# A transpose of 8192 x 8192 floats: ranges begun one step apart, TensorE's steps as a loop, neighbouring copies merged

## The chip, the cores and the metric

The kernel runs on one core of a Trainium2 chip. The metric is the device time in microseconds (us). Each execution lists its time, the core's span (first to last instruction) and the share of the TensorE clock that was granted.

## The reference

```python
x = np.random.randn(8192, 8192).astype(np.float32)
def reference(x):
    return np.transpose(x)
```

It reads 268 MB and writes 268 MB. There is no arithmetic, so the work is moving bytes: in, turned by TensorE in 128 x 128 blocks, out.

## The kernel before

The matrix is cut into two strips of 4096 columns. A step takes 128 rows of a strip: one load of 2 MB (16 KB in each of 128 partitions), 32 transposes into PSUM (the memory that TensorE writes its results to, here eight banks), and copies from there into output registers, which are SBUF buffers of 2 MB. The strip has eight ranges of 512 columns. A range fills one register with the blocks of eight steps, so that a store writes rows of 4 KB. There are three input buffers and nine registers: eight are being filled, and one or two are on their way to memory.

```python
S = 32; B = 4; W = 8; NR = S // B     # 8 ranges of 4 blocks; 8 steps fill a register
NIN = 3; NREG = 9; NPS = 8
nc.alloc_sbuf_tensor("pad", [P, 32], dt)                 # 128 bytes, never used
pss = [nc.alloc_psum_tensor(f"ps{k}", [P, B * P], dt).ap() for k in range(NPS)]
...
for t, (s, c) in enumerate(chunks):
    nc.tensor.wait_ge(s_ld[t % NIN], 16 * (t // NIN + 1))
    for q in [(c + k) % NR for k in range(NR)]:          # the turn: a new register comes last
        if q not in window:
            end = min(c + (q - c) % W, CH - 1)           # a window never crosses a strip's end
            r = free.pop(0)
            ...  # the copying engine waits until register r has been stored
        if bank[n % NPS] is not None:
            nc.tensor.wait_ge(*bank[n % NPS])            # one of eight banks
        ...  # 4 transposes into ps, then one copy of 128x512 on ScalarE or VectorE
    for q, e, count in closing:
        ...  # wait for the copy, then store the register
    if t + NIN < len(chunks):
        nc.sync.wait_ge(s_pe, n)
        load(t + NIN)                                    # the load goes out after the store
```

The turn puts the range that needs a newly returned register last in its step. PSUM is handed back bank by bank. In the queue of DMA transfers each step's store goes ahead of the next load.

## Time and profile before

| reading | value | view |
|---|---|---|
| time, median of 3 | 1268.06 us (1265.97 to 1268.59) | times |
| span of the profiled run | 1265.1 us | page |
| busy: TensorE, VectorE, ScalarE | 722.6, 353.5, 300.7 us | page, part 1 |
| a packet of 16 KB on one DMA engine | 611 ns | packet records |
| a 2 MB load, a 2 MB store, issue to landing (the last of its 16 completion records) | 23.5, 22.7 us | page, part 6 |

The first lines are from the page of the kernel before: TensorE's busy time, DMA share and rate in 40 slices of the span, and the packets that bring instructions.

```profile
PE 722.6 (57%) x4096; PEld 690.6 (55%) x4096; DVE 353.5 (28%) x512; ACT 300.7 (24%) x513; POOL 0.7 (0%) x6
...
DMA  9999999999999999999999999999999999999998
GB/s 380 418 428 427 428 429 428 427 428 428 426 428 429 426 428 430 429 428 428 428 417 428 428 427 428 431 429 429 429 428 428 430 428 430 429 429 429 428 428 353
...
q8 instruction: 32, 0.52, 0.2%
```

DMA is at 9 tenths or more nearly to the end, while TensorE has 43% of the span left. Sixteen engines at 16,384 bytes in 611 ns make 429.0 GB/s. I use that as the full rate. The **loss** of a stretch is its length minus its bytes divided by the full rate, from the packet records (instruction packets are not counted as bytes moved). It comes out a little below zero where packets overlap.

Next, the windows view of the kernel before. Columns: stretch in us; its length; busy time (and instructions) of TensorE, its weight loads, VectorE, ScalarE and GpSimd; granted clock; DMA share; GB/s.

```profile
0.00:50.00 50.00, 32.62 (x224) 31.70 (x224) 18.71 (x28) 17.49 (x29) 0.70 (x6) 0.90 0.97 393
50.00:600.00 550.00, 319.98 (x1792) 306.70 (x1792) 155.50 (x225) 131.21 (x224) 0.00 (x0) 0.75 1.01 428
600.00:700.00 100.00, 55.66 (x320) 50.94 (x320) 27.14 (x40) 23.14 (x40) 0.00 (x0) 0.69 1.01 425
850.00:1150.00 300.00, 175.18 (x989) 167.82 (x987) 85.77 (x124) 72.64 (x124) 0.00 (x0) 0.76 1.01 429
1150.00:1240.00 90.00, 52.61 (x288) 50.48 (x288) 24.90 (x36) 21.09 (x36) 0.00 (x0) 0.73 1.01 429
```

And its last ten microseconds:

```profile
1255.00:1260.00 5.00, 0.00 (x0) 0.00 (x0) 0.00 (x0) 0.00 (x0) 0.00 (x0) 0.50 0.80 323
1260.00:1265.00 5.00, 0.00 (x0) 0.00 (x0) 0.00 (x0) 0.00 (x0) 0.00 (x0) 0.50 0.22 87
```

The rate is 428 to 429 GB/s except at the start, around the change of strips (600 to 700 us) and at the end, where the share falls to 0.80 and 0.22 because the sixteen engines don't finish together. In the middle TensorE waits for loads, as the waits view says (who waited for whom: us in total, times, longest):

```profile
PE ps L131 <- DMA in<-in_x_dram: 499.7, 124, 8.3
...
ACT reg L142 <- DMA out_dram<-reg: 33.8, 6, 13.5
DVE reg L144 <- DMA out_dram<-reg: 33.4, 5, 18.1
```

The queue is deep. The DMA part of the page gives issues, their size, and the median us from issue to landing; at 4.9 us for 2 MB, 23 us is nearly five transfers:

```profile
in<-in_x_dram SPq DMA_DIRECT2D x128, 2048.0 KB, 23.5
out_dram<-reg SPq DMA_DIRECT2D x114, 2048.0 KB, 22.7
```

One step on the timeline of the kernel before (start, length, engine, instruction, and in brackets the idle time before it and what ended it):

```profile
383.82 0.34 SPq L98 DMA_DIRECT2D in<-in_x_dram  x1
...
388.16 6.06 PE L131 MATMUL ps<-ident,in 128*128 128x128 f32 x32 [4.37 <-DMA in<-in_x_dram]
...
390.04 0.55 SPq L28 DMA_DIRECT2D out_dram<-reg  x1
...
394.25 0.34 SPq L98 DMA_DIRECT2D in<-in_x_dram  x1
```

A load lands, TensorE starts at once, the step's store is issued 1.9 us later and the next load when TensorE is done.

### The profile page before, as it was taken

Reading aid. Unit: us, or ns where it says so; the run is one execution under the profiler, and the core shown is the slowest. Engines: PE = TensorE matmul, PEld = TensorE weight load, DVE = VectorE, ACT = ScalarE, POOL = GpSimd, SP = SyncE. Lnnn points to the kernel's source line nnn. Section 1 sums busy time; section 2 is a strip of 40 time slices with the busy share of each in tenths; the row PEclk is TensorE's granted clock in tenths of the full one; section 3 lists DMA queues with packets and bytes.
Section 4 is the critical chain, followed back from the end, with each engine's and each line's share of the span. In section 5 each row is a group of like instructions: output and inputs, shape, how many; then the busy total and the mean of one; then the engine's idle time right before and its main releaser. Section 6 shows DMA issues by size and latency. Waiting matters only on the chain.

```text
span 1265.1 us, 9814 instructions
## 1 busy us (share of the span) xinstructions
PE 722.6 (57%) x4096; PEld 690.6 (55%) x4096; DVE 353.5 (28%) x512; ACT 300.7 (24%) x513; POOL 0.7 (0%) x6
## 2 busy tenths in 40 slices
PE   6555656665556555565456655656566555665651
PEld 6555645555456555564455555655455555565551
DVE  3322222322223222232133322223223222232220
ACT  3322222222222222222122222222222222222220
POOL 0000000000000000000000000000000000000000
PEclk8877686777776877768667777686867877777675
DMA  9999999999999999999999999999999999999998
GB/s 380 418 428 427 428 429 428 427 428 428 426 428 429 426 428 430 429 428 428 428 417 428 428 427 428 431 429 429 429 428 428 430 428 430 429 429 429 428 428 353
DMA packets 39308, 537.51 MB, mean 425 GB/s; under 512 B 4320, under 2 KB 4832, under 8 KB 6240
## 3 DMA queue, kind: packets, MB, share of 16 engines
q1 hardware_dynamic: 39264, 536.89, 100.0%
q8 instruction: 32, 0.52, 0.2%
q14 instruction: 12, 0.10, 0.0%
HBM read 268.44 MB, written 268.44 MB: 424 GB/s over the span
## 4 chain that ended last, share of the span: by engine, by line
DMA 78%; PE 20%; issue 0%; DVE 0%; ACT 0%; SPq 0%; ACTq 0%
DMA in<-in_x_dram 75%; PE ps L131 20%; DMA out_dram<-reg 2%; DVE reg L144 0%; ACT reg L142 0%; SPq L197 0%; SPq L68 0%; ACTq L140 0%
## 5 line engine op out<-in xcount | busy, mean ns | idle before, releaser
L131 PE MATMUL ps<-ident,in 128*128 128x128 f32 x4096 | 722.6, 359 | 514.8 <-DMA in<-in_x_dram 499.7
L131 PEld LDWEIGHTS ps<-ident,in 128*128 128x128 f32 x4096 | 690.6, 193 | 546.5 <-DMA in<-in_x_dram 520.8
L144 DVE COPY reg<-ps 128x512 f32<-128x512 f32 x512 | 353.5, 692 | 884.2 <-PE ps L131 850.8
L142 ACT COPY reg<-ps 128x512 f32<-128x512 f32 x512 | 299.4, 586 | 936.5 <-PE ps L131 902.7
L142 ACT ACT_TABLE_LOAD x1 | 1.3, 1283 | 0.9 <-SPq L68 0.9
L83 POOL TENSOR_SCALAR_AFFINE_SELECT ident<-ident 128x128 f32<-128x128 f32 x1 | 0.3, 292 | 0.2 <-POOL ident L81 0.2
L81 POOL MEMSET ident<- 128x128 f32 x1 | 0.2, 204 | 0.5 <-SPq L68 0.5
L186 POOL MEMSET const-bfloat16-1.0<- 128x1 bf16 x1 | 0.1, 101 | 0.0
L186 POOL MEMSET const-uint8-127<- 128x1 uint8 x1 | 0.1, 101 | 0.0
L186 POOL MEMSET const-float32-0.0<- 128x1 f32 x1 | 0.1, 98 | 0.2 <-issue 0.2
L186 POOL MEMSET const-float32-1.0<- 128x1 f32 x1 | 0.1, 98 | 0.0
## 6 DMA issues: line engine op xcount, KB each, us to landing
in<-in_x_dram SPq DMA_DIRECT2D x128, 2048.0 KB, 23.5
out_dram<-reg SPq DMA_DIRECT2D x114, 2048.0 KB, 22.7
out_dram<-reg SPq DMA_DIRECT2D x4, 1792.0 KB, 20.1
out_dram<-reg SPq DMA_DIRECT2D x4, 1536.0 KB, 19.2
out_dram<-reg SPq DMA_DIRECT2D x4, 1280.0 KB, 19.1
out_dram<-reg SPq DMA_DIRECT2D x4, 1024.0 KB, 17.9
out_dram<-reg SPq DMA_DIRECT2D x4, 768.0 KB, 16.3
out_dram<-reg SPq DMA_DIRECT2D x4, 512.0 KB, 13.2
```

Source lines behind the costliest of these rows:

```text
L81: nc.gpsimd.memset(ident, 0.0).then_inc(s_id, 1)
L83: nc.gpsimd.affine_select(out=ident, in_=ident, compare_op=mybir.AluOpType.not_equal, fill=1.0, base=0, pattern=[[-1, P]], channel_multipl ...
L131: last = nc.tensor.transpose(ps[:, b * P:(b + 1) * P], ins[t % NIN][:, (q * B + b) * P:(q * B + b + 1) * P], ident,)
L142: cp = nc.scalar.copy(out=o, in_=i)
L144: cp = nc.vector.tensor_copy(out=o, in_=i)
L186: nc = _bacc.Bacc("TRN2", target_bir_lowering=False, num_devices=1)
```

## The change

The intent: before, all ranges restart at the head of a strip, so that TensorE runs short of work at the seam and short stores pile up there. Now range q begins q steps after range 0 and takes its rows round (the last ones at the head of the strip), so that the strips join without a seam. TensorE's program becomes a loop of three steps. Copies of neighbouring ranges become one instruction. The core of the diff (cuts marked):

```diff
-        nc.alloc_sbuf_tensor("pad", [P, 32], dt)
-        pss = [nc.alloc_psum_tensor(f"ps{k}", [P, B * P], dt).ap() for k in range(NPS)]
+        pss = [nc.alloc_psum_tensor(f"ps{h}", [P, NH * R], dt).ap() for h in range(2)]
...
+    for t in range(T):                       # T = 2 * 64 + 7 steps
+        at = sorted(((t - q) // CH, q) for q in range(NR) if t >= q)
+        active.append([a for a in at if a[0] < NS])
...
+    EARLY = 2 * NIN                          # the first six loads have a place each
+    after = [None] * EARLY + [2, 4, 5] + list(range(6, T))
+    order = [("L", t) for t in range(9)]
+    for t in range(6, T):
+        if t + NIN < T:
+            order.append(("L", t + NIN))     # the load now goes ahead of the step's store
+        if closing[t]:
+            order.append(("S", t))
...
+        def transposes(t):
+            ...
+            for h in range((n + NH - 1) // NH):          # halves of four ranges, in column order
+                if used[h]:
+                    nc.tensor.sem_inc(s_bank[h], -1).wait_op(s_bank[h], 1, "sem-ge")
+                ...                                      # up to 16 transposes into half h
+        with nc.Fori(0, len(full) // NIN, engines=[nc.tensor.engine]):
+            for t in range(first, first + NIN):
+                transposes(t)
...
+                eng = (nc.scalar, nc.vector)[h]          # half 0: ScalarE, half 1: VectorE
+                ...                                      # one copy for up to four ranges
```

PSUM is now two halves of four banks. A half goes back to TensorE when all of its copies are done.

More of the change, by code (lines that the diff above doesn't have):

```diff
@@ L56 @@
     dt = x.dtype
-    S = 32
     B = 4
-    W = 8
-    NR = S // B
+    NR = 8
+    NH = NR // 2
     NIN = 3
-    NREG = 9
-    NPS = 8
+    NREG = NR + 1
     CH = N // P
-    J = S * P
+    R = B * P
+    J = NR * R
+    NS = M // J
+    T = NS * CH + NR - 1
+    SIZE = NR * R
+    active = []
+    for t in range(T):
+        at = sorted(((t - q) // CH, q) for q in range(NR) if t >= q)
+        active.append([a for a in at if a[0] < NS])
+    window_of = {}
+    closing = [None] * T
+    for s in range(NS):
+        for q in range(NR):
+            for t0 in range(s * CH + q, s * CH + q + CH, NR):
+                t1 = t0 + NR - 1
+                parts = []
+                a = t0
+                for t in range(t0, t1 + 1):
+                    if t == t1 or (t + 1) % CH == 0:
+                        parts.append((a, t))
+                        a = t + 1
+                w = {"col": s * J + q * R, "t0": t0, "t1": t1, "parts": parts}
+                closing[t1] = w
+                for t in range(t0, t1 + 1):
+                    window_of[t, s, q] = w
@@ new lines @@
+    free = list(range(NREG))
+    stored = [0] * NREG
+    for t in range(T):
+        for a in active[t]:
+            w = window_of[(t, *a)]
+            if w["t0"] == t:
+                w["reg"] = free.pop(0)
+                w["before"] = stored[w["reg"]]
+        if closing[t]:
+            stored[closing[t]["reg"]] += len(closing[t]["parts"])
+            free.append(closing[t]["reg"])
+    EARLY = 2 * NIN
+    after = [None] * EARLY + [2, 4, 5] + list(range(6, T))
+    order = [("L", t) for t in range(9)]
@@ L68 @@
+    for t in range(6, T):
+        if t + NIN < T:
+            order.append(("L", t + NIN))
+        if closing[t]:
+            order.append(("S", t))
     with tc.tile_critical():
-        nc.alloc_sbuf_tensor("pad", [P, 32], dt)
         ident = nc.alloc_sbuf_tensor("ident", [P, P], dt).ap()
         ins = [nc.alloc_sbuf_tensor(f"in{k}", [P, J], dt).ap() for k in range(NIN)]
-        regs = [nc.alloc_sbuf_tensor(f"reg{k}", [P, B * W * P], dt).ap() for k in range(NREG)]
-        pss = [nc.alloc_psum_tensor(f"ps{k}", [P, B * P], dt).ap() for k in range(NPS)]
+        regs = nc.alloc_sbuf_tensor("regs", [P, NREG * SIZE], dt).ap()
+        pss = [nc.alloc_psum_tensor(f"ps{h}", [P, NH * R], dt).ap() for h in range(2)]
@@ L75, with home @@
         s_id = nc.alloc_semaphore("s_id")
+        s_early = [nc.alloc_semaphore(f"s_early{t}") for t in range(EARLY)]
         s_ld = [nc.alloc_semaphore(f"s_ld{k}") for k in range(NIN)]
         s_st = [nc.alloc_semaphore(f"s_st{k}") for k in range(NREG)]
+        s_bank = [nc.alloc_semaphore(f"s_bank{h}") for h in range(2)]
         s_pe = nc.alloc_semaphore("s_pe")
         s_cp = [nc.alloc_semaphore("s_cpa"), nc.alloc_semaphore("s_cpv")]
+        def home(t):
+            buf, off = [
+                (ins[0], 0), (ins[0], R), (ins[0], 3 * R), (regs, (NREG - 1) * SIZE),
+                (ins[1], 0), (ins[2], 0),
+            ][t] if t < EARLY else (ins[t % NIN], 0)
+            return buf[:, off:off + len(active[t]) * R]
@@ L91 @@
         ).then_inc(s_id, 1)
-        nc.tensor.wait_ge(s_id, 2)
-        chunks = [(s, c) for s in range(M // J) for c in range(CH)]
-        def load(t):
-            s, c = chunks[t]
-            nc.sync.dma_start(
-                out=ins[t % NIN], in_=x[c * P:(c + 1) * P, s * J:(s + 1) * J]
-            ).then_inc(s_ld[t % NIN], 16)
-        for t in range(NIN):
-            load(t)
-        n = 0
-        copied = [0, 0]
-        bank = [None] * NPS
-        free = list(range(NREG))
-        stored = [0] * NREG
@@ L110 @@
-        window = {}
-        stores = 0
-        for t, (s, c) in enumerate(chunks):
-            nc.tensor.wait_ge(s_ld[t % NIN], 16 * (t // NIN + 1))
-            closing = []
-            for q in [(c + k) % NR for k in range(NR)]:
-                if q not in window:
-                    end = min(c + (q - c) % W, CH - 1)
-                    r = free.pop(0)
-                    window[q] = (c, end, r)
-                    if stored[r]:
-                        (nc.scalar, nc.vector)[q % 2].wait_ge(s_st[r], 16 * stored[r])
-                c0, end, r = window[q]
-                rows = (end - c0 + 1) * P
-                view = regs[r][:, :B * rows].rearrange("p (b i) -> p b i", b=B)
-                ps = pss[n % NPS]
-                e = q % 2
-                if bank[n % NPS] is not None:
-                    nc.tensor.wait_ge(*bank[n % NPS])
-                for b in range(B):
-                    last = nc.tensor.transpose(
-                        ps[:, b * P:(b + 1) * P],
-                        ins[t % NIN][:, (q * B + b) * P:(q * B + b + 1) * P],
+        used = [False, False]
@@ new lines, in transposes @@
+        def transposes(t):
+            if t < EARLY:
+                nc.tensor.wait_ge(s_early[t], 16)
+            else:
+                nc.tensor.sem_inc(s_ld[t % NIN], -16).wait_op(s_ld[t % NIN], 16, "sem-ge")
+            src = home(t)
+            n = len(active[t])
+            for h in range((n + NH - 1) // NH):
+                if used[h]:
+                    nc.tensor.sem_inc(s_bank[h], -1).wait_op(s_bank[h], 1, "sem-ge")
+                used[h] = True
+                for b in range(min(NH, n - h * NH) * B):
+                    tr = nc.tensor.transpose(
+                        pss[h][:, b * P:(b + 1) * P],
+                        src[:, h * NH * R + b * P:h * NH * R + (b + 1) * P],
@@ L134 @@
                         ident,
                     )
-                last.then_inc(s_pe, 1)
-                n += 1
-                o = view[:, :, (c - c0) * P:(c - c0 + 1) * P]
-                i = ps.rearrange("p (b i) -> p b i", b=B)
-                (nc.scalar, nc.vector)[e].wait_ge(s_pe, n)
-                if e == 0:
-                    cp = nc.scalar.copy(out=o, in_=i)
-                else:
-                    cp = nc.vector.tensor_copy(out=o, in_=i)
-                cp.then_inc(s_cp[e], 1)
@@ L146 @@
-                copied[e] += 1
-                bank[(n - 1) % NPS] = (s_cp[e], copied[e])
-                if c == end:
-                    closing.append((q, e, copied[e]))
-            for q, e, count in closing:
-                c0, end, r = window.pop(q)
-                rows = (end - c0 + 1) * P
-                j0 = s * J + q * B * P
-                dst = out[j0:j0 + B * P, c0 * P:c0 * P + rows]
-                dst = dst.rearrange("(b q) i -> q b i", q=P)
-                nc.sync.wait_ge(s_cp[e], count)
-                if stores:
-                    st = wide_dma(nc, nc.sync, "qSPDynamicHW", dst, regs[r][:, :B * rows])
-                else:
-                    st = nc.sync.dma_start(
-                        out=dst, in_=regs[r][:, :B * rows].rearrange("q (b i) -> q b i", b=B)
-                    )
-                st.then_inc(s_st[r], 16)
-                stores += 1
-                stored[r] += 1
-                free.append(r)
@@ L167 @@
-            if t + NIN < len(chunks):
-                nc.sync.wait_ge(s_pe, n)
-                load(t + NIN)
+                tr.then_inc(s_pe, 1)
+        nc.tensor.wait_ge(s_id, 2)
+        full = [t for t in range(T) if len(active[t]) == NR]
+        first = full[0] + len(full) % NIN
+        for t in range(first):
+            transposes(t)
+        with nc.Fori(0, len(full) // NIN, engines=[nc.tensor.engine]):
+            for t in range(first, first + NIN):
+                transposes(t)
@@ new lines @@
+        for t in range(full[-1] + 1, T):
+            transposes(t)
+        n = 0
+        done = []
+        copied = [0, 0]
+        final = [max(t for t in range(T) if len(active[t]) > h * NH) for h in range(2)]
+        over = []
+        for t in range(T):
+            for h in range((len(active[t]) + NH - 1) // NH):
+                eng = (nc.scalar, nc.vector)[h]
+                ws = [window_of[(t, *a)] for a in active[t][h * NH:(h + 1) * NH]]
+                place = []
+                for w in ws:
+                    if w["t0"] == t and w["before"]:
+                        eng.wait_ge(s_st[w["reg"]], 16 * w["before"])
+                    a, z = next(p for p in w["parts"] if p[0] <= t <= p[1])
+                    off = w["reg"] * SIZE + (a - w["t0"]) * R + (t - a) * P
+                    place.append((off, (z - a + 1) * P))
+                runs = []
+                for g in range(len(ws)):
+                    if runs:
+                        u = runs[-1]
+                        d = place[g][0] - place[g - 1][0]
+                        if place[g][1] == place[u[0]][1] and abs(d) < 2 ** 15 and (
+                            len(u) == 1 or d == place[u[1]][0] - place[u[0]][0]
+                        ):
+                            u.append(g)
+                            continue
+                    runs.append([g])
+                ends = [w is closing[t] for w in ws]
+                if any(ends) and len(runs) == 1 and len(ws) > 1:
+                    half = len(ws) // 2
+                    runs = [runs[0][:half], runs[0][half:]]
+                runs.sort(key=lambda u: not any(ends[g] for g in u))
+                n += 1
+                eng.wait_ge(s_pe, n)
+                for u in runs:
+                    off, dist = place[u[0]]
+                    dims = [list(regs.ap[0]), [dist, B], [1, P]]
+                    i = pss[h][:, u[0] * R:(u[-1] + 1) * R]
+                    if len(u) > 1:
+                        dims.insert(1, [place[u[1]][0] - off, len(u)])
+                        i = i.rearrange("p (l b i) -> p l b i", l=len(u), b=B)
+                    else:
+                        i = i.rearrange("p (b i) -> p b i", b=B)
+                    o = bass.AP(regs.tensor, regs.offset + off, dims)
+                    cp = nc.scalar.copy(out=o, in_=i) if h == 0 else nc.vector.tensor_copy(out=o, in_=i)
+                    if any(ends[g] for g in u):
+                        cp.then_inc(s_cp[h], 1)
+                        copied[h] += 1
+                        closing[t]["copied"] = [(s_cp[h], copied[h])]
+                        if u is runs[-1] and t < final[h]:
+                            eng.wait_ge(s_cp[h], copied[h])
+                            eng.sem_inc(s_bank[h], 1)
+                    elif u is runs[-1] and t < final[h]:
+                        cp.then_inc(s_bank[h], 1)
+                    elif u is runs[-1]:
+                        cp.then_inc(s_cp[h], 1)
+                        copied[h] += 1
+                        over.append((t, (s_cp[h], copied[h])))
+            done.append(n)
@@ new lines @@
+        stores = 0
+        for what, t in order:
+            if what == "L":
+                if after[t] is not None:
+                    nc.sync.wait_ge(s_pe, done[after[t]])
+                s, q = active[t][0]
+                j0 = s * J + q * R
+                i0 = t % CH * P
+                nc.sync.dma_start(
+                    out=home(t), in_=x[i0:i0 + P, j0:j0 + len(active[t]) * R]
+                ).then_inc(s_early[t] if t < EARLY else s_ld[t % NIN], 16)
+                continue
+            w = closing[t]
+            for c in w["copied"] + [c for k, c in over if k < t]:
+                nc.sync.wait_ge(*c)
+            for a, z in w["parts"]:
+                rows = (z - a + 1) * P
+                i0 = a % CH * P
+                dst = out[w["col"]:w["col"] + R, i0:i0 + rows]
+                dst = dst.rearrange("(b q) i -> q b i", q=P)
+                base = w["reg"] * SIZE + (a - w["t0"]) * R
+                src = regs[:, base:base + B * rows]
+                if stores:
+                    st = wide_dma(nc, nc.sync, "qSPDynamicHW", dst, src)
+                else:
+                    st = nc.sync.dma_start(out=dst, in_=src.rearrange("q (b i) -> q b i", b=B))
+                st.then_inc(s_st[w["reg"]], 16)
+                stores += 1
```

## The prediction

> **What bounds the kernel now.** The DMA engines. The page shows 9 tenths or more in every slice but the last. The windows view gives a DMA share of 1.00 to 1.02 in every 40 us stretch sampled, and 0.98 to 1.05 across the seam between strips (610 to 660 us), at 399 to 439 GB/s. So the seam starves TensorE (granted clock 0.50, PE 1.1 busy us of 5), not the DMA. In the packet records a 16 KB packet takes 611 ns: 536.9 MB in such packets over 16 engines is 32768 x 0.611 / 16 = 1251 us (estimate). The queue's packet times sum to 1264.5 us per engine; the span is 1265.1. The rest has slack: per step of 9.9 us (1265/128), PE is busy 5.6, VectorE 2.8, ScalarE 2.3 (page, part 1). The chain of waits is 78% DMA; its 20% PE are passages where DMA is busy too.
>
> **What can be won:**
> - start: first packet at 2.0 us; unchanged;
> - small stores at the seams, about 2.7 us over full rate (2 KB packets take 91 ns, 8 KB about 320);
> - stretched packets, mostly in the first 60 us: 2 to 3 us;
> - TensorE's program: 32 instruction packets of 16 KB (8192 PE instructions x 64 B; DMA part of the page). The Trainium skill, "Runtime: NRT & Kernel Launch", section "Instruction fetch mechanics", says that the sequencer streams its program by DMA in 16 KiB blocks; the trace agrees. Cost: 32 x 0.611 / 16 = 1.2 us (estimate);
> - tail: DMA share 0.80 at 1255 to 1260, 0.22 at 1260 to 1265. A load's 16 landings spread over 0.3 us at the start, 6 us near the end: engines drift apart, probably by those instruction packets; worth about 3 us.
>
> **What the change does.**
> - Staggered ranges: same bytes. Each strip's short stores (1 to 7 blocks of 256 KB, seven ranges) come back as windows split where rows wrap: again 28, so the 2.7 us stay. 14 loads become partial (2 to 14 KB packets): +1.3 us (estimate, half of 2.7: 14 against 28). TensorE no longer idles at the seam: worth nothing, DMA was full.
> - PE loop: instruction packets fall to a handful, -1 us; less drift, tail -2 us. That page's section warns that a taken branch can force a fetch; even 2 us (estimate) per three steps would hide in PE's slack.
> - Merged copies: 4 x 586 ns to about 1.9 us, 4 x 692 to about 2.3 us (estimates). No time: both engines are under 30% busy. PSUM becomes two halves, and half a step of PE (2.8 us) overlaps the other half's copy.
> - Load before store in the queue: a register's previous store lands later relative to its load, but two to three transfers (10 us or more) stay queued behind it. No starvation in the steady state.
> - Ramp: reads alone deliver 2 MB in 4.9 us, PE's cold step takes 6.5 us: a bubble of 0 to 2 us around 30 us. First store by the plain form, 4 KB packets: +0.4 us.
>
> **Sum:** -1 -2 +1.3 +0.4 +0.7, calmer packets early -1: about -2 us. Predicted 1266 us, 8 in 10 between 1259 and 1272. Faster by over 2% 0.01, within 2% 0.97, slower 0.02.
>
> **What would show it:** DMA share still 1.00 throughout; instruction packets 0.05 to 0.15 MB; fewer, longer copies; PE without the seam hole; landings spread under 3 us near the end; last slice nearer 380 GB/s.
>
> **What would make it wrong:** instruction refetches stalling PE beyond its slack; copies waiting for stores (returned registers) letting DMA share fall to 0.95; slow strided merged copies.

## The result, and the profile after

Ratios are the mean time of one kernel's fast runs over the mean of the other's in the same rounds, so they are not quite the ratio of the medians quoted.

The changed kernel takes **1283.25 us** (1278.85 to 1286.09, 4 runs), the kernel before 1268.32 (the three executions above and a fourth). The ratio is 1.0117, 95% interval 1.0082 to 1.0152. It is within 2%, but on the wrong side of the forecast, outside its range, and well clear of noise. Run again beside the first experiments (`after_again`, below) the ratio was 1.0124.

The page of the changed kernel:

```profile
PE 710.3 (56%) x4096; PEld 675.6 (53%) x4096; DVE 290.7 (23%) x221; ACT 257.7 (20%) x293; POOL 0.7 (0%) x6
...
DMA  8999999999999999999999999999999999999997
GB/s 353 406 427 429 430 430 429 430 430 429 428 431 430 429 431 430 429 431 427 422 411 431 430 429 431 429 427 430 427 426 430 417 420 430 418 429 408 406 407 311
...
q8 instruction: 3, 0.05, 0.0%
```

The instruction packets are gone, as intended (3 for 32). But the first slices are slower, and from the 32nd slice on the rate falls to between 406 and 430. Its windows, to be read against those of before:

```profile
0.00:50.00 50.00, 30.31 (x208) 27.15 (x208) 10.55 (x6) 15.64 (x12) 0.70 (x6) 0.92 0.94 366
50.00:600.00 550.00, 312.48 (x1806) 298.23 (x1807) 129.12 (x103) 110.42 (x123) 0.00 (x0) 0.75 1.01 429
600.00:700.00 100.00, 55.90 (x308) 53.57 (x306) 23.60 (x14) 17.78 (x25) 0.00 (x0) 0.73 1.01 421
850.00:1150.00 300.00, 166.24 (x962) 158.61 (x963) 70.79 (x51) 58.94 (x56) 0.00 (x0) 0.75 1.01 425
1150.00:1240.00 90.00, 55.80 (x309) 53.51 (x308) 20.68 (x25) 20.47 (x39) 0.00 (x0) 0.73 1.00 408
```

Its last ten microseconds with data:

```profile
1265.00:1270.00 5.00, 0.00 (x0) 0.00 (x0) 0.00 (x0) 0.00 (x0) 0.00 (x0) 0.50 0.77 322
1270.00:1275.00 5.00, 0.00 (x0) 0.00 (x0) 0.00 (x0) 0.00 (x0) 0.00 (x0) 0.50 0.06 26
```

A share of 0.06 is one engine of sixteen: for the last five microseconds a single one is still working. Added up as losses, the two profiled spans differ by this:

| stretch, us | loss before | loss after | difference |
|---|---|---|---|
| 0 to 50 (ramp) | 4.3 | 7.3 | +3.1 |
| 50 to 600 | 1.9 | -0.2 | -2.1 |
| 600 to 700 (seam) | 1.1 | 1.9 | +0.8 |
| 700 to 850 | 0.4 | -0.1 | -0.4 |
| 850 to 1240 | 0.4 | 7.2 | +6.8 |
| 1240 to the end | 5.7 | 9.4 | +3.8 |
| sum | | | +12.0 |

The sum is the difference of the spans, 1277.1 - 1265.1 (differences were rounded after subtraction). So there is a gain of about 2 us in the middle, and three losses: ramp, late stretch, tail.

The waits have changed their nature. In the changed kernel:

```profile
ACT regs L242 <- DMA out_dram<-regs: 591.7, 55, 20.4
PE ps L177 <- PEq L174: 543.1, 146, 9.0
DVE regs L242 <- DMA out_dram<-regs: 511.8, 64, 11.2
...
PE ps L177 <- DMA in<-in_x_dram: 3.8, 1, 3.8
```

The copies wait for stores, 592 and 512 us where it was 34 and 33. TensorE hardly waits for loads any more (4 us against 500) but 543 us at L174, which is the line where it takes back a PSUM half (PEq is TensorE's own instruction sequencer, which does the waiting). And a transfer is landed sooner, that is, fewer stand in the queue:

```profile
in<-in_x_dram SPq DMA_DIRECT2D x121, 2048.0 KB, 18.1
out_dram<-regs SPq DMA_DIRECT2D x114, 2048.0 KB, 18.9
```

About 5 us less than before for a load is one transfer less. The timeline of the changed kernel has the new chain:

```profile
385.58 1.86 ACT L242 COPY regs<-ps 128x2048 f32<-128x2048 f32 x1 [7.92 <-DMA out_dram<-regs]
...
387.59 5.08 PE L177 MATMUL ps<-ident,in 128*128 128x128 f32 x32 [3.26 <-PEq L174]
...
392.70 0.34 SPq L267 DMA_DIRECT2D in<-in_x_dram  x1
...
395.50 2.36 DVE L242 COPY regs<-ps 128x1024 f32<-128x1024 f32 x2 [8.77 <-DMA out_dram<-regs]
...
398.00 4.24 PE L177 MATMUL ps<-ident,in 128*128 128x128 f32 x25 [3.09 <-PEq L174]
```

A store lands (its register is free), the copy that was waiting for it runs, the half of PSUM comes back, TensorE works, and only then the next load goes out. Before, TensorE followed the loads, and only the last copy of a step could ever wait for a register. (The chain-of-waits view can't be used after: it follows 0% of the span through the counted-down semaphores.)

**The ramp.** The first steps have one to four ranges and so use half 0 alone:

```profile
11.59 1.44 ACT L242 COPY regs<-ps 128x1536 f32<-128x1536 f32 x1 [2.98 <-PE ps L177]
...
13.18 1.94 PE L177 MATMUL ps<-ident,regs 128*128 128x128 f32 x16 [1.62 <-PEq L174]
15.15 1.86 ACT L242 COPY regs<-ps 128x2048 f32<-128x2048 f32 x1 [2.12 <-PE ps L177]
...
17.16 3.32 PE L177 MATMUL ps<-ident,in 128*128 128x128 f32 x20 [2.05 <-PEq L174]
```

TensorE and ScalarE take turns and don't overlap. The eighth load waits for TensorE's fifth step, which ends at 20.5 us, and the queue has run dry by then:

```profile
20.00:25.00 5.00, 3.81 (x19) 3.43 (x18) 0.69 (x1) 1.53 (x1) 0.00 (x0) 0.50 0.78 279
```

**The late stretch.** Each transfer leaves 16 completion records, one for each engine. They give the spread between the first and the last of the 16, and I take means over the transfers of a stretch. Before, it was 2.3 us in the first 150 us, 4.2 between 450 and 600, 5.9 between 1000 and 1150. After, it was 1.7, 5.9 and 9.5, and of those 9.5 us the very last engine alone made 6.4. When one engine is that late, the others are up to 9 us ahead of the landing that everything waits for, in a queue of only 18 us, and theirs run short. In the packet records, nine packets of 1.2 us (mean of those of 0.8 us or more) begin from 1157.0 us on, 1.0 us after a load was issued, as the very first packets of the kernel before begin 1.0 us after its first issue and take about 1.3 us. Another 30 begin between 1160 and 1164 us, in the middle of transfers, and 34 between 1188.7 and 1195 us. In all, the time of 16 KB packets above 611 ns makes 7.6 us per engine from 850 to 1240 us, about the whole loss. The share hides it, because a stretched packet counts as busy. That a queue is empty is not shown here: in this stretch each next transfer was issued at least 1.3 us before the foremost engine's completion record. Why packets stretch when the queue is that short, some of them in mid-transfer, stays open. This is the changed kernel at 99% share:

```profile
1160.00:1165.00 5.00, 5.00 (x25) 5.00 (x24) 0.00 (x0) 0.00 (x0) 0.00 (x0) 0.50 0.99 328
```

### The profile page after: what moved, and what is told of

Read it like the earlier page. It is cut to its first block, busy times and chain, and to the rows that moved or that the text cites. A ratio compares the mean times of both kernels' runs of the same rounds, so it can differ in the third digit from the quotient of the medians.

```text
span 1277.1 us, 9643 instructions
## 1 busy us (share of the span) xinstructions
PE 710.3 (56%) x4096; PEld 675.6 (53%) x4096; DVE 290.7 (23%) x221; ACT 257.7 (20%) x293; POOL 0.7 (0%) x6
## 5 line engine op out<-in xcount | busy, mean ns | idle before, releaser
L177 PE MATMUL ps<-ident,in 128*128 128x128 f32 x4080 | 708.3, 354 | 545.3 <-PEq L174 541.5
L177 PEld LDWEIGHTS ps<-ident,in 128*128 128x128 f32 x4080 | 673.9, 190 | 579.2 <-issue 578.7
L242 DVE COPY regs<-ps 128x512 f32<-128x512 f32 (+3 forms) x221 | 290.7, 1351 | 944.0 <-DMA out_dram<-regs 511.8
L242 ACT COPY regs<-ps 128x512 f32<-128x512 f32 (+3 forms) x292 | 256.4, 937 | 999.1 <-DMA out_dram<-regs 591.7
## 6 DMA issues: line engine op xcount, KB each, us to landing
in<-in_x_dram SPq DMA_DIRECT2D x121, 2048.0 KB, 18.1
```

The costliest lines, as they stand in the source:

```text
L177: tr = nc.tensor.transpose(pss[h][:, b * P:(b + 1) * P], src[:, h * NH * R + b * P:h * NH * R + (b + 1) * P], ident,)
L242: cp = nc.scalar.copy(out=o, in_=i) if h == 0 else nc.vector.tensor_copy(out=o, in_=i)
```

## The experiments

"Spread" below is the mean spread of landings between 1000 and 1150 us, "late loss" the loss from 850 to 1240 us, "ramp" the loss of the first 50 us, each from the profiled run. All kernels gave the right result.

| run | what | median us | ratio to before (95%) | load to landing, us | spread, us | ramp / late loss / tail, us |
|---|---|---|---|---|---|---|
| before | | 1266 to 1268 | 1 | 23.5 | 5.9 | 4.3 / 0.4 / 5.7 |
| after_again | the change | 1283.09 | 1.0124 (1.0107, 1.0141) | 18.1 | 9.5 | 10.6 / 7.3 / 10.1 |
| store_first | after, store before load | 1276.57 | 1.0083 (1.0065, 1.0100) | 22.6 | 9.4 | 7.2 / 2.4 / 9.4 |
| unrolled | after, no loop | 1276.15 | 1.0070 (1.0053, 1.0087) | 18.1 | 9.1 | 8.1 / 2.7 / 8.2 |
| before_load_first | before, load before store | 1268.41 | 1.0010 (0.9993, 1.0027) | 22.9 | 6.4 | 4.1 / 0.6 / 6.3 |
| after_pad | after, 128 bytes back | 1275.13 | 1.0060 (1.0031, 1.0089) | 18.1 | 8.5 | 10.8 / 1.8 / 8.8 |
| before_no_pad | before, 128 bytes out | 1270.05 | 1.0036 (0.9996, 1.0077) | 23.4 | 6.2 | 4.2 / 0.5 / 5.4 |
| early_seventh | after, ramp's 8th load freed | 1281.13 | 1.0112 (1.0088, 1.0136) | 18.1 | 9.4 | 5.2 / 8.4 / 9.1 |
| store_first_unrolled | both | 1273.75 | 1.0053 (1.0031, 1.0076) | 22.6 | 8.1 | 6.3 / 1.5 / 6.6 |
| stagger_fine | stagger with before's machinery | 1267.61 | 1.0003 (0.9986, 1.0019) | 22.9 | 7.8 | 4.5 / 1.4 / 5.7 |
| unmerged | after, one copy a range | 1283.48 | 1.0138 (1.0114, 1.0163) | 18.0 | 9.2 | 8.0 / 7.6 / 9.4 |
| fine_fixed_order | stagger_fine, no turn | 1270.31 | 1.0016 (0.9993, 1.0039) | 20.7 | 9.1 | 3.8 / 2.4 / 7.3 |
| turn_by_fours | stagger_fine, banks by fours | 1269.44 | 1.0014 (0.9989, 1.0039) | 20.3 | 8.8 | 3.9 / 1.8 / 7.1 |
| best_loop | after, three repairs | 1267.33 | 1.0006 (0.9987, 1.0024) | 22.5 | 4.6 | 5.2 / 0.1 / 4.8 |
| best_loop_again | the same, 5 rounds | 1268.51 | 1.0015 (1.0001, 1.0029) | 22.4 | 5.0 | 9.4 / -0.1 / 5.1 |
| best_unrolled | best_loop, no loop | 1272.23 | 1.0042 (1.0028, 1.0055) | 22.4 | 8.5 | 10.9 / 0.9 / 6.8 |
| best_fine | stagger_fine, three repairs | 1267.35 | 1.0002 (0.9985, 1.0018) | 23.8 | 7.6 | 3.8 / 1.4 / 5.4 |
| pad_early | best_loop, load first | 1274.54 | 1.0047 (1.0020, 1.0074) | 18.2 | 6.7 | 9.4 / 2.2 / 8.8 |
| store_first_early | best_loop, 128 bytes out | 1274.91 | 1.0052 (1.0022, 1.0083) | 22.6 | 9.5 | 7.9 / 2.8 / 10.0 |

### First call: order, loop, or neither

Theory A: the order of the queue. Theory B: the loop. Theory C: the merged copies and the two halves.

**store_first**, the changed kernel with the queue's order of before:

```diff
-        if t + NIN < T:
-            order.append(("L", t + NIN))
         if closing[t]:
             order.append(("S", t))
+        if t + NIN < T:
+            order.append(("L", t + NIN))
```

> The changed kernel with only the order of the queue put back: each step's store is issued before the next load. Theory A (with the load first, a step's copies wait for a store that stands behind a load, so one input buffer sits full and the queue holds one transfer less: median 18 us from issue to landing instead of 23; once one DMA engine lags by 6 to 10 us the others run dry): back to about 1267 us, within 0.4% of the kernel before, landing near 23 us, VectorE and ScalarE waits for stores below 150 us each. Theory B (the TensorE loop, or the one engine that lags) and theory C (merged copies with PSUM in two halves): still 1278 us or more.

1276.57 us: 6.5 us of 16 came back. Between the profiles, the late stretch gives 4.9 us (7.3 to 2.4). Loads again stay 22.6 us in the queue. Ramp (7.2 us) and tail (9.4) are as in the first profile of the changed kernel (7.3 and 9.4); the ramp of its second, 10.6, shows how much a ramp differs from run to run. Theory A holds for a part. VectorE's waits for stores are gone, but ScalarE's only fell to 449 us: TensorE still waits for PSUM halves (521 us).

**unrolled**, the loop written out:

```diff
-        with nc.Fori(0, len(full) // NIN, engines=[nc.tensor.engine]):
-            for t in range(first, first + NIN):
-                transposes(t)
-        for t in range(full[-1] + 1, T):
+        for t in range(first, T):
             transposes(t)
```

> The changed kernel with only the TensorE loop written out again. Theory A: still 1277 to 1286 us; the instruction packets return (about 30 of 16 KB). Theory B (the loop costs, or its missing instruction packets let one engine lag): back under 1272 us, and the gap of the last landing to the one before it, 6 us late in the changed kernel, goes below 2 us.

1276.15 us, which neither theory had. The 33 instruction packets return and cost what they should (50 to 600 us loses 2.0 us instead of -0.2), yet the late loss falls to 2.7. The last landing is now about 1.6 us behind the one before it instead of 6.4, though the whole spread is still 9.1.

**before_load_first**, the order of the changed kernel in the kernel before (the load moves ahead of the loop over closing ranges):

> The kernel before with only the order of the queue changed: the next load is issued ahead of the step's stores, as in the changed kernel. Theory A: slower than the kernel before, by 4 to 15 us, landing near 18 us instead of 23, copies waiting several hundred us for stores. Theories B and C (loop or merged copies are the cause): same as the kernel before within 2 us.

1268.41 us, ratio 1.0010: a miss for theory A as I had put it. The copies do wait for stores (477 and 517 us), but a load still stays 22.9 us in the queue and a store even 27.5. The order alone does not shorten the queue. I concluded that it takes something that turns a waiting copy into a waiting TensorE; the third and fourth calls test that.

**after_again**, for comparison on the same chip:

> The changed kernel again, unaltered, on the same chip as the three others, as their point of comparison: 1278 to 1286 us by every theory.

1283.09 us, as expected.

### Second call: the 128 bytes, the ramp, and both repairs together

The change also dropped the unused 128-byte tensor. From the allocator's addresses, an input buffer began at byte 67 x 256 of a partition before and begins at 66.5 x 256 after. The Trainium skill, "DMA: Bandwidth & Descriptors", section "How a descriptor splits into AXI transactions", says that a descriptor that doesn't start on a 256-byte boundary is read from the boundary below it and so costs extra beats. The trace doesn't show that for a packet (611 ns for 16 KB in both kernels), but it might bear on the drift.

**after_pad**:

```diff
+        nc.alloc_sbuf_tensor("pad", [P, 32], dt)
         ident = nc.alloc_sbuf_tensor("ident", [P, P], dt).ap()
```

> The changed kernel with the unused 128-byte tensor put back ahead of the identity, so that all buffers start on a 256-byte boundary of a partition's memory as in the kernel before; nothing else. Theory D (without it each 16 KB row is off the boundary, and that makes one DMA engine fall behind by 1 us in about 120): the gap of the last landing to the one before it stays under 2 us late in the run, the rate stays near 428 GB/s to the end, loss after 850 us falls from 7 to under 2 us, tail from 9.5 to under 6.5: about 1272 us. Rival (the drift has another cause): 1278 to 1286 us, gap 6 us as in the changed kernel.

1275.13 us. The late loss fell from 7.3 to 1.8 us. The spread went only from 9.5 to 8.5 us, the last engine's own part of it from 6.4 to 3.3, and the tail stayed at 8.8. The boundary helps the time, but the drift less than theory D said.

**before_no_pad** (the same tensor taken out of the kernel before):

> The kernel before without its unused 128-byte tensor. Theory D: one engine falls behind here too (spread of a transfer's 16 landings near 9 us late in the run instead of 6), 2 to 6 us slower; its queue is deep enough that no slice falls below 425 GB/s. Rival: same as before within 1 us, spread 6 us.

Inconclusive: two of four runs were at 1266 us, two at 1274 to 1276. The profiled one was a quick one, with the spread and losses of the kernel before; the two long ones have no profile, so what the 128 bytes do to the kernel before stays open.

**early_seventh**, the ramp (the fifth load goes to register 7, so that the eighth load needs no wait):

```diff
-                (ins[1], 0), (ins[2], 0),
+                (regs, (NREG - 2) * SIZE), (ins[2], 0),
-    after = [None] * EARLY + [2, 4, 5] + list(range(6, T))
+    after = [None] * EARLY + [2, None, 5] + list(range(6, T))
```

> The changed kernel with one buffer of the ramp moved: the fifth load goes to the eighth, still unused output register, so the eighth load is issued behind the seventh instead of waiting for TensorE's fifth step. Theory (the ramp runs dry at 20 us because that load waits): the first 50 us lose 4 to 5 us against full rate instead of 7 to 10; 3 to 5 us faster than the changed kernel, 1274 to 1280 us. Rival (cold TensorE limits the ramp anyway): the gap moves from 20 to about 25 us and nothing is gained.

1281.13 us. In this profile the gap at 20 us is gone and the ramp loses 5.2 us. But the same repair in `pad_early`, `store_first_early`, `best_loop_again` and `best_unrolled` shows a gap at 25.5 us instead, and 7.9 to 10.9 us lost. So the rival expectation was the better one: the bubble moves.

**store_first_unrolled**, both of the first call's edits:

> The changed kernel with both the order of the queue put back and the TensorE loop written out. If the queue's depth and the lag of one engine act on the same loss late in the run (each alone took it from 7 to about 2.4 us), both together can only remove the 2.4 us left: 1272 to 1275 us. If they are separate costs (6.5 and 7 us) they add: 1269 to 1271 us.

1273.75 us, in the range for gains that don't add. The late loss itself cannot be removed twice, and only 1.5 us of it is left. By the ratios it is less clear: added gains would give 1.0029, measured is 1.0053, and each of the ratios behind this is uncertain by about 0.002. In the profiled run, what is left against the kernel before is mostly ramp (+2.1 us), late loss (+1.1) and tail (+0.9).

### Third call: stagger without the new machinery

**stagger_fine** keeps the stagger, the ramp's loads, the load-first queue and the buffers, and takes from the kernel before: TensorE written out, eight banks released one by one, one copy a range on alternating engines, and the turn. Its core:

```diff
+            turn = sorted(range(len(active[t])), key=lambda g: (active[t][g][1] - t - 1) % NR)
+            for g in turn:
+                ...
+                ps = pss[n % 8]
+                if bank[n % 8] is not None:
+                    nc.tensor.wait_ge(*bank[n % 8])
```

> The changed kernel's staggered ranges, ramp, load-first queue and buffers, but with the machinery of the kernel before: TensorE written out, eight banks released one by one, one copy for each range, ranges taken in turn so that the one with the new register comes last. Theory C (PSUM in two halves and a fixed order make half a step, and so TensorE and the next load, wait for one returning register): issue to landing back to 23 us or more, loss after 850 us under 1.5 us instead of 7, total 1269 to 1274 us, what is left being ramp and tail. Rival (staggering itself, with the load first, is what costs): landing near 18 us, 1276 us or more.

1267.61 us, ratio 1.0003. The whole difference in time is gone, better than expected, although the load still goes first and the 128 bytes are missing. Its DMA part, waits and windows:

```profile
in<-in_x_dram SPq DMA_DIRECT2D x121, 2048.0 KB, 22.9
```

```profile
ACT regs L199 <- DMA out_dram<-regs: 528.1, 57, 11.1
DVE regs L199 <- DMA out_dram<-regs: 523.5, 57, 11.1
PEld ps L189 <- DMA in<-in_x_dram: 474.5, 132, 5.3
PE ps L189 <- DMA in<-in_x_dram: 446.0, 132, 5.0
```

```profile
0.00:50.00 50.00, 32.53 (x237) 29.86 (x238) 16.67 (x25) 19.45 (x32) 0.70 (x6) 0.93 0.97 391
...
1150.00:1240.00 90.00, 49.61 (x267) 45.71 (x268) 24.80 (x39) 17.60 (x32) 0.00 (x0) 0.77 1.01 425
```

The copies wait for stores as long as in the changed kernel (528 and 524 us). But TensorE waits for loads again, and the load stays 22.9 us in the queue. Here a copy's wait is harmless, since TensorE doesn't inherit it. The ramp too is that of the kernel before (391 GB/s against 393 before and 366 after), and from 1150 to 1240 us it has 425 GB/s where the changed kernel has 408.

**unmerged**, the changed kernel with a copy for each range:

```diff
-                    if runs:
+                    if False:
                         u = runs[-1]
```

> The changed kernel with every range copied by its own instruction, PSUM still in two halves, TensorE still a loop. If merging the copies is what lets one engine lag or empties the queue: 1272 us or less, spread of landings late in the run below 7 us. If it is a matter of halves, order and queue: same as the changed kernel within 4 us (1278 to 1287), copies' busy time up by 20 to 25%.

1283.48 us, the same as the change. Merging as such costs and gains nothing. My reading is that it counts when the half comes back, and that is with its last copy either way. VectorE's busy time rose by 6% only (308 for 291 us), less than I had expected.

**best_loop** joins three repairs of the changed kernel: store first, the 128 bytes, the freed eighth load. Loop, halves and merging stay.

> The changed kernel with three repairs: store before load, buffers on a 256-byte boundary, and the eighth load not waiting in the ramp; loop and merged copies kept. If the losses found (ramp 3 to 6 us, late dips 7 us) are separate and all removable: 1265 to 1269 us, within 0.3% of the kernel before; the tail of 9 us remains. If the lag of one engine only moves the loss elsewhere: 1272 us or more.

1267.33 us. The late loss is gone and the spread is 4.6 us, with loop, halves and merging in place. So none of these is slow by itself; the halves cost time only together with what was repaired here:

```profile
0.00:50.00 50.00, 27.89 (x211) 25.35 (x212) 10.55 (x6) 17.63 (x15) 0.70 (x6) 0.96 0.96 384
...
1150.00:1240.00 90.00, 50.81 (x276) 48.07 (x274) 18.32 (x23) 22.10 (x43) 0.00 (x0) 0.73 1.01 427
```

**best_fine**, stagger_fine with the same three:

> Staggered ranges with the fine banks and the turn of the kernel before, plus the three repairs. If staggering gains anything when its side effects are gone: 1262 to 1266 us. If staggering only exchanges the seam (1 us) for a ramp (1.3 us of small loads): 1266 to 1269 us, the same as the kernel before.

1267.35 us, ratio 1.0002: the stagger gains nothing even with these repairs.

### Fourth call: which part of the machinery, which repair

**fine_fixed_order** is stagger_fine with `turn = range(len(active[t]))`:

> The run stagger_fine (1267.6 us) with one thing taken from the changed kernel: the ranges of a step are taken in fixed order of their columns, so the one that waits for a returning register stands anywhere in the step. If the order is what ties TensorE to the returning store: a load's time from issue to landing falls from 23 to about 18 us, TensorE waits several hundred us for copies instead of loads, 1272 to 1280 us. If it is the halves: landing stays near 23, 1266 to 1270 us.

1270.31 us and 20.7 us in the queue, each at the edge between the two expectations. TensorE now waits for copies as well as for loads:

```profile
PE ps L189 <- ACT regs L199: 246.6, 58, 9.9
...
PE ps L189 <- DMA in<-in_x_dram: 162.0, 81, 4.1
```

**turn_by_fours** is stagger_fine with the banks handed back in fours (TensorE waits, at each fourth range, for all copies of the group two before):

> The run stagger_fine with the other thing taken from the changed kernel: PSUM handed back four banks at a time, when all four copies are done; the turn, with the new register last, stays. If the halves are what ties TensorE to the returning store: landing near 18 us, 1272 to 1280 us. If it is the order: landing stays near 22 us or above, 1266 to 1271 us.

1269.44 us and 20.3 us in the queue. So each of the two, order and fours, takes about half of the depth that the changed kernel lost (22.9 to 20.7 and 20.3, where both together stand at 18.1), and costs 1 to 2 us by the ratios (1.0016 and 1.0014 against 1.0003), though neither is clear of the kernel before by its interval. The nearest run with both is `unrolled`, 9 us slower than the kernel before, far more than their sum. But it also merges copies (which `unmerged` acquits) and gives each half to one copying engine, where stagger_fine alternates the two. A run with exactly both, and one with only the engines bound to halves, were not made.

**pad_early** and **store_first_early** are best_loop less the order and less the 128 bytes:

> The run best_loop (1267.3 us) with its order of the queue undone: load before store, as in the changed kernel; 256-byte boundary and repaired ramp stay. If the order is worth what it was alone (6.5 us): 1271 to 1275 us, loss late in the run 1 to 3 us. If boundary and ramp are enough: 1266 to 1269 us.

> The run best_loop with its 256-byte boundary undone; store before load and repaired ramp stay. If the boundary lets one engine drift: spread of landings late in the run back near 9 us instead of 4.6, tail 9 us instead of 5, 1271 to 1275 us. If the boundary is irrelevant: 1265 to 1269 us, spread near 5 us.

1274.54 and 1274.91 us. Each of these two left out costs about 7 us against best_loop: late loss 2.2 and 2.8 us instead of 0, tail 8.8 and 10.0 instead of 5. Without the boundary the spread is back at 9.5 us, as expected. The ramp's repair was not left out alone.

### Fifth call: the loop by itself

> The run best_loop again, on another day's chip: its profile showed a spread of landings of only 4.6 us and a time of 1267.3 us, while leaving out either the order of the queue or the boundary gave 1274.5 and 1274.9. If those three were a real interaction: 1265 to 1269 us and a spread under 6 us again. If best_loop was luck of the drift: 1271 to 1276 us, spread 7 to 10 us.

1268.51 us, spread 5.0 us, on another chip: best_loop was no luck of the drift. An interaction in time is not needed to explain it, though: taken alone, the three repairs (store_first, after_pad, early_seventh) lowered the ratio by 0.0041, 0.0064 and 0.0012, together 0.0117, and best_loop lowered it by 0.0118. It is the spread that none of the three brought under 8.5 us alone. The ramp lost 9.4 us this time against 5.2.

> The run best_loop with TensorE's program written out. If the loop has a cost of its own (7 us in the changed kernel): 1259 to 1262 us, faster than the kernel before. If the loop costs only where one engine's lag meets a shallow queue: the same as best_loop within 2 us, 1266 to 1269 us, with some 30 instruction packets back.

1272.23 us, slower than either expectation. This profile has the poor ramp again:

```profile
0.00:50.00 50.00, 34.09 (x204) 31.22 (x205) 8.26 (x5) 15.64 (x12) 0.70 (x6) 0.97 0.86 336
```

Against best_loop_again, whose span is 4.9 us shorter, the ramp makes only about 1.5 us of the difference. The tail makes 1.7, the late stretch 1.0, and the stretch from 50 to 600 us 0.9 (it lost 0.8 us where the loop lost -0.1). The spread was 8.5 us again. So no cost of the loop itself shows here; it was the faster of the two. That the 7 us which writing it out brought in the changed kernel belonged to the drift meeting a shallow queue is my reading, not shown.

### What holds the late losses together

| spread, us | load to landing, us | late loss, us | runs |
|---|---|---|---|
| 9.2 to 9.5, 4.3 to 6.4 of it the last engine | 18 | 7.2 to 8.4 | after, after_again, early_seventh, unmerged |
| 6.7 to 9.1 | 18 | 1.8 to 2.7 | unrolled, after_pad, pad_early |
| 8.8 to 9.5 | 20 to 23 | 1.8 to 2.8 | store_first, store_first_early, fine_fixed_order, turn_by_fours |
| 7.6 to 8.5 | 22 to 24 | 0.9 to 1.5 | stagger_fine, best_fine, best_unrolled, store_first_unrolled |
| 4.6 to 6.4 | 22 to 24 | -0.1 to 0.6 | before, before_load_first, before_no_pad, best_loop twice |

A wide spread and a shallow queue together cost most, but the two numbers don't decide it: `unrolled`, with 9.1 and 18.1 us, lost only 2.7, and there the last engine's own part was 1.6 us. One number orders the runs better, the reserve of the foremost engine: by how much the next transfer's issue came before a transfer's first completion record (median from 850 to 1240 us, worked out from the traces afterwards). It is 4.2 to 4.5 us in the four runs that lost over 7 us, 4.7 to 6.1 in `unrolled`, after_pad, store_first_early and store_first (1.8 to 2.8 lost), 6.8 to 8.8 in five runs with 0.9 to 2.4 lost, and 9.8 to 13.2 in the other seven, with 1.4 or less. This is a correlation over single profiles; no run set the reserve by itself.

## Why the prediction was wrong

It said 1266 us (1259 to 1272); the kernel took 1283.25. Point by point:

- **DMA bounds the kernel: right.** Every loss and gain is in the DMA's rate.
- **The stagger's own effect, "worth nothing, DMA was full": right.** stagger_fine has a ratio of 1.0003, and the short stores and seam are as before (600 to 700 us loses 1.7 against 1.1 us).
- **Instruction packets, "-1 us": right in kind, and the gain was larger than forecast.** 3 packets for 32; the stretches from 50 to 600 and 700 to 850 us gained 2.1 and 0.4 us. The warning on branches in the Trainium skill ("Runtime: NRT & Kernel Launch", section "Instruction fetch mechanics"), which the prediction had named as a risk, didn't matter: no packets come back with the loop's 40 rounds.
- **Merged copies, "No time": right** (unmerged 1.0138 against 1.0124). A copy of four ranges took 1.87 us on ScalarE and 2.29 on VectorE, against 4 x 586 and 4 x 692 ns before.
- **"PSUM becomes two halves, and half a step of PE (2.8 us) overlaps the other half's copy": this step failed.** It holds only while both halves are in use and no copy waits; TensorE waited 543 us for halves, and 4 instead of 500 us for loads. In the ramp half 0 alone is in use, and TensorE and ScalarE alternate. In the steady state the half that holds a new register waits for a store, and TensorE and the next load wait with it. The prediction had counted TensorE's 43% of idle time as slack without asking what it would now wait for. That this wait shortens the queue is shown by stagger_fine (the loop and the merging, which it also drops, leave 18.1 and 18.0 us when they alone are dropped), which hands banks back singly with the new register last and has 22.9 us to landing again instead of 18.1, with the load still first. That the halves are enough to cost the time is not so: best_loop keeps them, with the store first and the 128 bytes back, and has a ratio of 1.0006.
- **"two to three transfers (10 us or more) stay queued behind it. No starvation in the steady state": failed late in the run.** The queue shrank by one transfer, as the time to landing shows (18.1 for 23.5 us), and that was enough until the engines had drifted apart. From 850 to 1240 us it cost 6.8 us.
- **"less drift, tail -2 us": the sign was wrong.** Fewer instruction packets did not mean less drift: with 3 of them the spread reached 9.5 us, with 32 it was 5.9 (best_loop, with 2, had 4.6). The tail cost +3.8 us.
- **"a bubble of 0 to 2 us around 30 us", counted as +0.7: the bubble came, the size was off, and the cause named (PE's cold step) was not the whole of it.** The bubble was at 20 us, where the eighth load waited for TensorE's alternation with ScalarE on half 0, and the ramp cost +3.1 us in one profile and +6.3 in the other (10.6 - 4.3). In the four kernels without fixed halves it lost 3.8 to 4.5 us, as before.

What led the sum astray was adding up small terms around a full queue and not asking how full the queue must be. The second item of the prediction's last paragraph ("copies waiting for stores ... letting DMA share fall to 0.95") names the mechanism. Late in the run, though, the share did not fall: it stayed at 1.00 from 1150 to 1240 us while the rate fell to 408 GB/s. It fell in the ramp (0.94 over the first 50 us) and in the tail.

**What stays open.** Why one engine lags, and why the 128 bytes, the order of the queue and the loop change that, is not settled. The records don't say which engine a packet ran on. The spread is wider than before from 300 us on (4.3 against 3.4 us between 300 and 450), long before anything is lost, so it is not a result of the losses. Taken alone in the changed kernel, the order acts on the depth (22.6 us to landing, spread still 9.4), the 128 bytes and the loop a little on the drift (8.5 and 9.1) and not on the depth (18.1). How they work together on the drift (4.6 in best_loop) is not shown. Nor did I find a ramp repair for two halves that holds from run to run.

## What to carry to other kernels

A kernel that keeps a queue full, as this one does, has its reserve in the depth of that queue, measured as time from issue to landing, not in the idle time of its engines; after a change, compare that time first, and the rate rather than the share. What kept the queue deep was to hand buffers back singly and to put the piece that waits for a slow return last (22.9 us in stagger_fine, 20.3 and 20.7 with only one of the two). The Trainium skill has advice on the instructions alone: "Perfetto Trace Analysis", section "Optimizing Scalar/DVE Operations", says that where unsaturated engines cause bubbles on others, "breaking up instructions may allow work to be completed sooner". Here breaking up the copies alone did nothing (`unmerged`, 1.0138 against 1.0124). No version here beats the kernel before: at 1266 to 1268 us against 1251 for its bytes at full rate, what is left is start, tail and seam.

## What the Trainium skill lacked or had wrong

- "DMA: Bandwidth & Descriptors", section "Latency and other measured facts", has two engines usually slower than the others and, as a best guess, calls it specific to transfers issued from GpSimd. Here every data transfer was issued from the sync engine, and between 1000 and 1150 us the last engine still landed 6.4 us behind the next slowest (which one, and whether it was always the same, the records don't say). The page's section "Why a DMA increments its semaphore by 16 and not by 1" says that the engines of a transfer finish independently; no page that I read says that the gap between them grows along a stream, here from 2.3 to 5.9 us before and from 1.7 to 9.5 us after.
- "Perfetto Trace Analysis", section "Identifying the Most-Contended Engine", says to use HBM utilization instead of occupancy for DMA, since sixteen engines make occupancy misleading. It lacks the reason seen here: stretched packets of 16 KB took 1.2 us (mean) instead of 0.611 and counted as busy, so the share stood at 0.99 where the rate was 328 GB/s.
- "Runtime: NRT & Kernel Launch", section "Instruction fetch mechanics", gives the fetch that a taken branch forces, when its target isn't in the prefetched window, as a reason to unroll fully. It isn't contradicted: the loop of three steps is about 12 KB (estimate: 192 instructions, at 32 packets of 16 KB for 8192) and showed no fetch per round. What it lacks is the other side: in this kernel, full on DMA, 40 rounds of the loop brought 3 instruction packets in place of 32 and about 2 us between 50 and 600 us.
- "DMA: Bandwidth & Descriptors", section "How a descriptor splits into AXI transactions", gives extra beats for a read that starts off a 256-byte boundary. Here a 16 KB packet took 611 ns (median) either way. What changed with 128 bytes was the drift (spread 9.5 and 4.6 us in store_first_early and best_loop) and 0.5% of the time; the kernel before, in its one profile without them, had 6.2 for 5.9 us.
